# A two-block model on one core: first loads, mLSTM rows, modulation, norms, out-projections and the pooling row rearranged

## The chip, the cores and the metric

The kernel runs on one core of one Trainium2 chip. The metric is the device time of one execution in microseconds, the median of the runs. Three runs of the kernel before took 828.54, 823.75 and 828.04 us, so the median is 828.04. The trace that is read here is of another execution, which took 830.03 us; the span of its work is 828.2 us.

## The reference

The model takes `x` of 256 tokens by 1024 features through six layers, all in fp32, and ends with a norm. Every weight is read once.

```python
def first_block(x, ...):                      # two layers, plain residuals
    x = x + even_layer(rms_norm(x, norm_w[0]), ...)   # mLSTM (4 heads of 128) and sparse attention
    x = x + hgrn2_layer(rms_norm(x, norm_w[1]), ...)  # 8 gated recurrent heads of 128
def second_block(x, c, ...):                  # two layers, modulated by c
    c_act = jax.nn.silu(c)
    for i in range(2):
        mod = c_act @ ada_w[i] + ada_b[i]     # 1024 x 6144
        sh1, sc1, g1, sh2, sc2, g2 = jnp.split(mod, 6, axis=-1)
        h = modulate(rmsnorm(x, norm_mix_g[i]), sh1, sc1)
        x = x + g1 * (pool_mixer if i == 0 else sgu_mixer)(h, ...)
        h = modulate(rmsnorm(x, norm_mlp_g[i]), sh2, sc2)
        x = x + g2 * (jnp.square(jax.nn.relu(h @ w1)) @ w2)   # 1024 -> 4096 -> 1024
    return rmsnorm(x, final_g)
```

`even_layer` projects to some 4,400 columns and an out-projection of 1024 by 1024 ends it. The mLSTM works in chunks of 128 tokens; a product with exp(D - m) needs, for every head, the running maximum `m` and the summed gate `bcum`, one row of 256 numbers each, on all 128 partitions. The attention has 8 heads of 64 in two groups; its softmax rows are multiplied with the values of the selected blocks, of the window and of 15 compressed blocks. `pool_mixer` takes moving means over 2, 4, 8 and 16 tokens by four groups of 256 features and multiplies each group by a 256 by 256 matrix.

## The kernel before

**Tiles.** The residual stream `xT` lies with features on partitions: 8 tiles of 128 features by 256 tokens. A weight matrix is cut into pieces of 1024 by 128, laid out as 128x1024. SyncE's queue (SP) loads two of them at once (1 MB, `raw`, three buffers). Each fp32 piece is split (`split_w`, L155 to L163): ScalarE casts it to the matmul's rounded type (`whi`, L161), VectorE subtracts to get the low half (`wlo`, L162); four buffers each. Activations are split likewise into `ahi` and `alo` (or `num`, `nout`, `ghl`). A column tile is then 24 matmuls of 256 columns (`mm_T`, L221 to L223): hi by hi, hi by lo, lo by hi, for each of eight row tiles. Products that are not split run as plain fp32, two passes for each (x2 in the rows).

**Stages.** The even layer runs to about 208 us (35 column tiles in the order of the list `EV_TILES`, then an out-projection of 8 tiles), the recurrent layer to 343, pooling to 377, mlp0's two matrices to 465 and some 541, the sgu follows, then mlp1 from 637, then the last norm and four output transfers of 256 KB. In the even layer two generators, `mlstm` (one head a step) and `nsa` (the attention, in pieces), are called between column tiles with `run`, so that their work stands among the tiles' matmuls.

**Modulation.** `c_act @ ada_w` is done by VectorE: 96 loads of 512 KB (`araw`, two buffers, SP's queue), each reduced in one instruction against `row_c` (L351) into a column of `mod`, with a short read of the accumulator behind it. `ada` is a generator whose steps hold one or two of these; `step(upto)` issues the next one with a raised priority, `finish(upto)` all that are due. Calls of `step` stand in the stages by hand.

**Order.** A scheduler puts the instructions of each engine into a fixed order ahead of the run, by data dependencies, buffers and priorities; on the chip every engine works through its list and waits where an operand isn't there. PSUM has three banks for column tiles (`gbank`) and two for everything else (`mbank`).

**Places that the change touches.** The first loads stand at L106 to L109 and L175. A norm adds up seven squares on VectorE and sends two products of all ones through TensorE (L294). The mLSTM's selecting products read `mrow` and `bcum`, tensors of 4 partitions (L557, L559, L578); behind them come the mask products L558, L560 and the products by `ones` (L575, L588). The attention's products with the values are L776 (64 columns of weights for a group, so half of the array's columns) and L777 (compressed blocks): for one head in turn, all of group 0, then all of group 1. Pooling builds `prow`, a row of 1024 numbers on all partitions, with eight products over a broadcast of `mod` (L977) and four copies (L978); `pz` (L993) reads it, and the band product (L998) reads `pz`. In mlp1 the last column tile goes through the same code as the others: 512-column matmuls (hi and lo of the activation side by side, L1035), 256-column ones (L1036), and then two adds into `xT` (L330), the second of a copied half (L1041).

Of the kernel before, what the change touches and what calls it, by code (L numbers as in the profile page):

```python
# [8 lines left out]
F32 = mybir.dt.float32  # L9
# [9 lines left out]
T = 256  # L19
KT = 8  # L20
# [45 lines left out]
def tile_kernel(ctx: ExitStack, tc: tile.TileContext, io: dict, out: bass.AP):  # L66
# [37 lines left out]
    norm_w = mk(base, [128, 16], F32, "norm_w")  # L104
    xT = mk(base, [128, KT, T], F32, "xT")
    nc.scalar.dma_start(norm_w, io["norm_w"])  # L106

    def load_x(k):
        nc.sync.dma_start(xT[:, k : k + 2, :], io["xT"][k // 2].rearrange("p (k t) -> p k t", k=2))  # L109


# [53 lines left out]
    class Weights:  # L165
# [5 lines left out]
        def first(self, c0, c1, src):  # L171

            if not self.raw:
                self.raw[0] = mk(wpool, [128, 2048], F32, "raw", bufs=3)
            nc.scalar.dma_start(self.raw[0][:, c0:c1], src)  # L175

        def ahead(self, i, n):

            self.split = {i: self.piece(i, n, True)}
# [10 lines left out]
    def tile_T(ps, w, i, pair):  # L190

        wh, wl = w.piece(i, 128)
        mm_T(ps, lambda k: wh[:, k, :], lambda k: wl[:, k, :], pair.hi, pair.lo, range(KT))

# [60 lines left out]
    class Norm:  # L255
# [27 lines left out]
        def square(self, k, i=None):  # L283
# [3 lines left out]
            if i < KT - 1:  # L287
# [25 lines left out]
    def out_proj(src, pair, evict, side=0, every=1):  # L313
        w = Weights(lambda c: src[c])
        for n in range(8):
            if every and n % every == 0:
                step(side)
            ps = gbank()[:, :T]
            tile_T(ps, w, n, pair)
            evict(n, ps)  # L320
# [17 lines left out]
    def ada(crow):  # L338
# [19 lines left out]
    done = [0]  # L358
# [32 lines left out]
    def even_layer(norm, nxt, w):  # L391
        with ExitStack() as es:
# [65 lines left out]
            def columns(names):  # L458
                for name in names:
# [8 lines left out]
                    ps = gbank()[:, :T]  # L468
# [12 lines left out]
            columns(EV_TILES[:6])  # L481
# [14 lines left out]
            th = mk(wpool, [128, 1024], F32, "araw", bufs=2)  # L496
# [22 lines left out]
            out_proj(io["ev_w_out"], y, add_x(nxt), 5, 2)  # L519

    def mlstm(ev, et, qk, v, gsb, num, tanh):
# [10 lines left out]
        bc = mk(ev, [4, T], F32, "bcum")  # L532
# [3 lines left out]
        mr = mk(ev, [4, T], F32, "mrow")  # L536
# [12 lines left out]
        for h in range(H):  # L549
# [9 lines left out]
            PE.matmul(pb[:, 256:384], sel, mr[:, 128:256], start=True, stop=False)  # L559
# [18 lines left out]
            PE.matmul(pm[:, 0:T], sel, bc, start=True, stop=True)  # L578
# [18 lines left out]
    def nsa(ev, et, nqk, sv, gsb, cpair, nout):  # L597
# [111 lines left out]
        for qb in range(2):  # L709
# [33 lines left out]
            for j in range(4):  # L743
# [13 lines left out]
                for g in range(2):  # L757
                    for b in range(2):
# [3 lines left out]
                        else:  # L762
                            S.mul(x, x, r)
                    pt = mbank(0)
                    nb = qb + 1
# [6 lines left out]
                    dst = pov[64 * g : 64 * g + 64, j, :]  # L772
# [187 lines left out]
    def pool_layer(band, mod, norm, nxt):  # L960


        with ExitStack() as es:
# [7 lines left out]
            z = mk(pp, [128, 2, 1024], F32, "pz")  # L971
            for g in range(4):
                cs = slice(g * 256, g * 256 + 256)
                ps = mbank()[:, :256]
                for i in range(2):
                    k = 2 * g + i
                    PE.matmul(ps, mod[:, k : k + 1].to_broadcast([128, 128]), raw[:, k, :], start=i == 0, stop=i == 1)  # L977
                S.copy(row[:, cs], ps)  # L978
# [367 lines left out]
```

## Time and profile before

| | |
|---|---|
| median of three runs | 828.04 us |
| profiled execution | 830.03 us |
| its span | 828.2 us |
| TensorE busy | 807.2 us (97%), 6534 matmuls |
| weight loads | 740.2 us (89%) |
| VectorE | 672.1 us (81%) |
| ScalarE | 520.3 us (63%) |
| GpSimd | 4.9 us (1%) |
| DMA | 184.64 MB, mean 223 GB/s |

Matmuls are pipelined: a row's duration reaches into the next row's, so the price of one is the step from its start to the next start. "Idle before" is the time that an engine stood still ahead of a group, with what ended it. A chain of waits that goes back from the last instruction lies on TensorE for 66 per cent of the span, on DMA for 13 and on VectorE for 12.

### The profile page before, as it was taken

How to read it: one execution, taken by the hardware profiler on the slowest of the kernel's cores; microseconds unless marked ns; L12 is line 12 of the kernel's file. 1: busy time of each engine (PE TensorE's matmuls, PEld its weight loads, DVE VectorE, ACT ScalarE, POOL GpSimd, SP SyncE). 2: the span in 40 equal slices, each digit the busy share in tenths (PEclk: the TensorE clock that was granted, in tenths of full speed). 3: DMA queues.
4: the chain of work that ended last, by engine and by line, in shares of the span. 5: the costliest groups of instructions: out<-in, count | busy, mean ns of one | idle time of the engine just before them, and what ended most of it. 6: DMA issues, size and time to landing. Idle time of an engine off the chain costs nothing.

```text
span 828.2 us, 16357 instructions
## 1 busy us (share of the span) xinstructions
PE 807.2 (97%) x6534; PEld 740.2 (89%) x6534; DVE 672.1 (81%) x1257; ACT 520.3 (63%) x934; POOL 4.9 (1%) x19
## 2 busy tenths in 40 slices
PE   8999999989999999999999999999999999999995
PEld 8968977879999987999999888889999999988884
DVE  7689988899899989999999888876679777755552
ACT  7556765676876556658776734446657777754441
POOL 0000000001000000000000000000000000000000
PEclk9999999999999999999999999999999999999998
DMA  9644566657885777568878889874445454555521
GB/s 345 254 168 144 185 224 221 236 198 251 293 290 204 249 255 258 203 231 271 293 278 285 287 314 316 310 265 154 160 146 204 153 203 163 195 187 175 198 102 51
DMA packets 34635, 184.64 MB, mean 223 GB/s; under 512 B 3968, under 2 KB 4608, under 8 KB 19200
## 3 DMA queue, kind: packets, MB, share of 16 engines
q1 hardware_dynamic: 33696, 181.96, 62.8%
q10 hardware_dynamic: 864, 1.65, 0.6%
q8 instruction: 51, 0.84, 0.4%
q14 instruction: 24, 0.20, 0.1%
HBM read 182.55 MB, written 1.05 MB: 222 GB/s over the span
## 4 chain that ended last, share of the span: by engine, by line
PE 66%; DMA 13%; DVE 12%; ACT 5%; issue 4%; DVEq 0%; ACTq 0%; SPq 0%
PE g L221 12%; PE g L222 12%; DMA araw<-in_ada_w_dram 12%; PE g L223 12%; PE g L1035 9%; PE g L1036 5%; DVE wlo L162 4%; DVE araw L351 3%; ACT whi L161 2%; PE g L207 1%; PE g L208 1%; PE g L206 1%; PE m L858 1%; PE m L748 1%; PE long L776 1%
## 5 line engine op out<-in xcount | busy, mean ns | idle before, releaser
L221 PE MATMUL g<-ahi,whi 128*128 128x258 f32 (+1 forms) x1256 | 360.1, 289 | 4.0 <-ACT ahi L213 2.5
L222 PE MATMUL g<-alo,whi 128*128 128x258 f32 (+1 forms) x1256 | 357.6, 286 | 0.1
L223 PE MATMUL g<-ahi,wlo 128*128 128x258 f32 (+1 forms) x1256 | 356.6, 285 | 0.0
L162 DVE TENSOR_TENSOR wlo<-raw,whi 128x1024 fp32r<-128x1024 f32 (+1 forms) x238 | 288.6, 1216 | 73.5 <-ACT whi L161 72.9
L161 ACT CAST whi<-raw 128x1024 fp32r<-128x1024 f32 (+1 forms) x238 | 246.2, 1043 | 160.1 <-PE g L222 68.0
L221 PEld LDWEIGHTS g<-ahi,whi 128*128 128x128 f32 x1256 | 238.7, 191 | 8.7 <-ACT ahi L213 3.1
L222 PEld LDWEIGHTS g<-alo,whi 128*128 128x128 f32 x1256 | 240.2, 191 | 2.1 <-issue 0.8
L223 PEld LDWEIGHTS g<-ahi,wlo 128*128 128x128 f32 x1256 | 239.3, 191 | 1.7 <-issue 1.0
L1035 PE MATMUL g<-ghl,whi 128*128 128x512 f32 x512 | 179.9, 394 | 0.6 <-DVE nb L1020 0.6
L1036 PE MATMUL g<-ghl,wlo 128*128 128x256 f32 x512 | 143.5, 280 | 2.7 <-DVE wlo L162 2.4
L351 DVE CUSTOM_DVE_ANT_0 araw<-araw,row_c,prm 128x1024 f32<-128x1024 f32 x96 | 122.5, 1279 | 23.5 <-DMA araw<-in_ada_w_dram 23.3
L1035 PEld LDWEIGHTS g<-ghl,whi 128*128 128x128 f32 x512 | 96.0, 187 | 23.3 <-issue 0.7
L1036 PEld LDWEIGHTS g<-ghl,wlo 128*128 128x128 f32 x512 | 96.0, 187 | 4.0 <-DVE wlo L162 3.9
L310 DVE TENSOR_TENSOR nt<-g,nrstd 128x256 f32<-128x256 f32 x133 | 55.5, 419 | 17.3 <-PE g L223 16.9
L1021 ACT ACTIVATE nt<-nt,nb 128x256 f32<-128x256 f32 x64 | 32.4, 507 | 21.3 <-DVE nb L1020 21.3
L280 ACT ACTIVATE ahi<-xT,gains 128x256 fp32r<-128x256 f32 x32 | 16.2, 507 | 36.2 <-DVE xT L330 32.3
L214 DVE TENSOR_TENSOR ghl<-nt,ghl 128x256 fp32r<-128x256 f32 x64 | 27.0, 423 | 3.8 <-ACT ghl L213 1.4
L1022 ACT ACTIVATE nt<-nt 128x256 f32<-128x256 f32 x64 | 26.7, 418 | 1.9
L213 ACT CAST ghl<-nt 128x256 fp32r<-128x256 f32 x64 | 25.9, 406 | 1.9
L208 PE MATMUL g<-wlo,ahi 128*128 128x512 f32 (+1 forms) x64 | 24.3, 379 | 0.0
L206 PE MATMUL g<-whi,ahi 128*128 128x512 f32 (+1 forms) x64 | 24.2, 378 | 0.0
L286 ACT ACTIVATE sq<-xT 128x256 f32<-128x256 f32 x56 | 22.3, 405 | 3.0 <-DVE xT L330 3.0
(290 smaller groups left out, 758.7 us busy)
## 6 DMA issues: line engine op xcount, KB each, us to landing
raw<-in_mlp_w_dram SPq DMA_DIRECT2D x64, 1024.0 KB, 5.0
araw<-in_ada_w_dram SPq DMA_DIRECT2D x96, 512.0 KB, 5.1
raw<-in_ev_w_in_dram SPq DMA_DIRECT2D x17, 1024.0 KB, 6.1
raw<-in_od_w_in_dram SPq DMA_DIRECT2D x16, 1024.0 KB, 6.0
raw<-in_sgu_w_in_dram SPq DMA_DIRECT2D x8, 1024.0 KB, 4.7
raw<-in_ev_w_out_dram SPq DMA_DIRECT2D x4, 1024.0 KB, 4.9
raw<-in_od_w_out_dram SPq DMA_DIRECT2D x4, 1024.0 KB, 4.9
raw<-in_sgu_w_out_dram SPq DMA_DIRECT2D x4, 1024.0 KB, 4.7
```

The lines of the kernel that those rows point to most:

```text
L161: S.copy(hi[:, c], r[:, c])
L162: V.tensor_sub(lo[:, c], r[:, c], hi[:, c])
L206: PE.matmul(ps[tb], pair.hi(k)[:, ts_], wh[:, j, :], start=st, stop=False)
L208: PE.matmul(ps[tb], pair.hi(k)[:, ts_], wl[:, j, :], start=False, stop=sp)
L221: PE.matmul(ps, wh(k), ah(k), start=st, stop=False)
L222: PE.matmul(ps, wh(k), al(k), start=False, stop=False)
L223: PE.matmul(ps, wl(k), ah(k), start=False, stop=sp)
L310: V.tensor_tensor(t, ps[:, :T], self.r, op=ALU.mult)
L351: V.tensor_tensor_reduce(raw, raw, crow, 1.0, P("ada_b", layer * 48 + c), ALU.mult, ALU.add, mod[:, c : c + 1])
L1021: S.activation(r, r, AF.Relu, bias=b)
L1035: PE.matmul(ps, wh[:, k, :], a.rearrange("p s t -> p (s t)"), start=st, stop=sp, skip_group_check=True)
L1036: PE.matmul(ps[:, :T], wl[:, k, :], a[:, 0, :], start=False, stop=sp, skip_group_check=True)
```

## The change

It has ten parts. (1) First loads: the weight halves of tiles 0 and 1 go by SP's queue, `x` with `norm_w` in front of it (one tensor `xn`) mostly by ScalarE's; tiles 1 and 2 are split ahead, and tiles 3 to 5 take `mbank`s. (2) `mrow` and `bcum` become 128 partitions high, zeros below the fourth, and the selecting products read all of them. (3) The attention's value products alternate between the two groups, the compressed blocks first. (4) Norms with a pair of operands add all eight squares on VectorE and send one product; the last norm keeps two. (5) An out-projection's first three tiles are done by row halves, in three banks, and no modulation step stands in it. (6) Modulation steps are called by a table of positions, `PACE`, in the mlps and the sgu, with three `araw` buffers. (7) An attention step moves ahead of four of the even layer's column tiles. (8) The pooling row is made by column-tiled products (32 columns of weights each, four side by side), copied once and spread over the partitions by four transfers on ScalarE's queue; the first band product takes 144 columns for 256. (9) mlp1's last tile is done by `mm_T`, without the copied half and the second add. (10) The output transfers alternate between SP's and ScalarE's queues.

```diff
+    def load_x(queue, k):
+        a = 0 if k == 0 else 16 + k * T
+        queue.dma_start(xn[:, a : 16 + (k + 2) * T], io["xn"] if k == 0 else io["xT"][k // 2 - 1])
+    def tiles_T3(ps, w, i, pair):
+        ws = [w.piece(i + j, 128) for j in range(3)]
+        for ks in (range(4), range(4, 8)):
+            for j in range(3):
+                wh, wl = ws[j]
+                mm_T(ps[j], ..., pair.hi, pair.lo, ks, ks[0] == 0, ks[0] == 4)
-                if i < KT - 2:
+                if i < KT - 1 - two:
-            PE.matmul(self.ps, ones, sq, start=i == KT - 2, stop=i == KT - 1)
+            PE.matmul(self.ps, ones, sq, start=i == KT - 2 or not two, stop=i == KT - 1)
-                        raw = mk(wpool, [128, 1024], F32, "araw", bufs=2)
+                        raw = mk(wpool, [128, 1024], F32, "araw", bufs=3)
+    PACE = ((0, 30), (256, 36), (512, 60), (640, 66), (704, 66), (960, 72))
+    def pace(tiles):
+        u = done[1]
+        done[1] += tiles
+        for (u0, s0), (u1, s1) in zip(PACE, PACE[1:]):
+            if u0 <= u < u1:
+                while done[0] * (u1 - u0) < s0 * (u1 - u0) + (s1 - s0) * (u - u0):
+                    step(12)
-            columns(EV_TILES[25:31])
+            columns(EV_TILES[25:27])
+            run(ns)
+            columns(EV_TILES[27:31])
...
-            run(ns)
-            out_proj(io["ev_w_out"], y, add_x(nxt), 5, 2)
+            out_proj(io["ev_w_out"], y, add_x(nxt))
+        bc128, mr128 = [mk(ev, [128, T], F32, t) for t in ("bcum", "mrow")]
+        G.memset(bc128, 0.0)
+        G.memset(mr128, 0.0)
-            sel = ident[0:4, h : h + 1].to_broadcast([4, 128])
+            sel = ident[:, h : h + 1].to_broadcast([128, 128])
-            PE.matmul(pb[:, 0:T], sel, mr, start=True, stop=False)
+            PE.matmul(pb[:, 0:T], sel, mr128, start=True, stop=False)
-                    for b in range(2):
-                        for i in range(nb):
-                            PE.matmul(dst, vv, pT[:, b, i, :], start=b == 0 and i == 0, stop=False, skip_group_check=True)
-                    PE.matmul(dst, vcp[:, g, j, :], ptc[:, g, :], start=False, stop=True, skip_group_check=True)
+                for g in range(2):
+                    PE.matmul(pov[64 * g : 64 * g + 64, j, :], vcp[:, g, j, :], ptc[:, g, :], start=True, stop=False, skip_group_check=True)
+                for b in range(2):
+                    for i in range(nb):
+                        for g in range(2):
+                            PE.matmul(pov[64 * g : 64 * g + 64, j, :], vv, pTs[g][:, b, i, :], start=False, stop=b == 1 and i == nb - 1, skip_group_check=True)
-                    PE.matmul(ps, mod[:, k : k + 1].to_broadcast([128, 128]), raw[:, k, :], start=i == 0, stop=i == 1)
-                S.copy(row[:, cs], ps)
+                    PE.matmul(ps[32 * g : 32 * g + 32], mod[:, k : k + 1].to_broadcast([128, 32]), raw[:, k, :], start=i == 0, stop=i == 1, tile_position=(0, 32 * g))
+            S.copy(row4, ps)
+                nc.scalar.dma_start(row[:, g * 256 : g * 256 + 256], row4[32 * g : 32 * g + 1, None, :].to_broadcast([1, 128, 256]))
-                PE.matmul(ps, z[:, 0, n * 128 : n * 128 + 128], m[:, 0:256], start=True, stop=False)
+                PE.matmul(ps[:, 0:144], z[:, 0, n * 128 : n * 128 + 128], m[:, 0:144], start=True, stop=False, skip_group_check=True)
-                if layer == 0 and n % 2 == 0:
-                    step(11)
-                if layer and n % 4 == 3:
-                    step(12)
+                pace(8)
+                    if layer and n == 7:
+                        mm_T(ps[:, :T], ..., range(8), first=c == 0, last=c == 3)
+                        continue
+    w.first(nc.sync, 0, 512, io["ev_w_0"][0])
+    load_x(nc.scalar, 0)
+    w.first(nc.sync, 512, 1024, io["ev_w_0"][1])
+    load_x(nc.scalar, 2)
+    load_x(nc.sync, 6)
+    load_x(nc.scalar, 4)
+    w.first(nc.sync, 1024, 2048, io["ev_w_1"])
-        nc.sync.dma_start(out[:, k : k + 2, :], x)
+        (nc.scalar if k % 4 else nc.sync).dma_start(out[:, k : k + 2, :], x)
```

What the scheduler makes of it is seen in the engines' lists. The first place is VectorE in the even layer, ahead of the low half `wlo_1715`, the 27th piece's (`araw` rows are modulation's reductions, `nmx` and `nsm` the attention's softmax, `w`, `qk` and `cpt` the mLSTM's). Before:

```order
L351 ISA araw_1333,mod_10_89<-araw_1333,row_c_396,prm_71 128x1024
L351 ISA mod_10_89 128x1
L162 TENSOR_TENSOR wlo_1715<-raw_1263,whi_1714 128x1024
L310 TENSOR_TENSOR nt_1293<-g_1262,nrstd_164 128x256
L569 SCALAR_TENSOR_TENSOR mE_1308<-m_231_1311,mE_1308 128x384
```

In the change:

```order
L787 RECIPROCAL nsm_892<-nsm_892 128x4
L615 TENSOR_TENSOR w_263_1447<-w_262_1445,w_263_1447 128x256
L788 TENSOR_TENSOR nsm_892<-nsm_892,gtok_703 128x4
L367 ISA araw_1620,mod_9_87<-araw_1620,row_c_394,prm_71 128x1024
L367 ISA mod_9_87 128x1
L793 TENSOR_SCALAR A_1376<-A_1376,nsm_892 128x128 x2
L621 SCALAR_TENSOR_TENSOR cpt_225_1296<-w_263_1447,m_265_1453 128x256
L586 SCALAR_TENSOR_TENSOR qk_181<-w_285_1533,qk_181 128x256
L586 SCALAR_TENSOR_TENSOR qk_181<-w_286_1536,qk_181 128x256
L757 TENSOR_REDUCE nmxc_1462<-m_272_1464 128x8
L163 TENSOR_TENSOR wlo_1715<-raw_1263,whi_1714 128x1024
```

`wlo_1715` was VectorE's instruction 169 and is now its 212th; between it and the piece before (`wlo_1266`) stand 11 reductions, where 3 stood.

The second place is TensorE at the attention's products with the values (`nPT` are the transposed softmax weights of one group, `sv` the values, `vcp` the compressed values; `m` and `kblk` belong to the scores of the next head). Before:

```order
L222 MATMUL g_1745<-alo_114,whi_1748 128x256
L776 MATMUL long_915<-nPT_1358,sv_175 64x128 x2
L777 MATMUL long_915<-nPtc_913,vcp_696 64x128
L776 MATMUL long_915<-nPT_1368,sv_175 64x128 x2
L777 MATMUL long_915<-nPtc_913,vcp_696 64x128
```

In the change:

```order
L814 MATMUL long_915<-nPT_1360,sv_183 64x128
L780 MATMUL m_247_1377<-kblk_663,nqk_185 128x256
L814 MATMUL long_915<-nPT_1365,sv_183 64x128
L814 MATMUL long_915<-nPT_1360,sv_183 64x128
L814 MATMUL long_915<-nPT_1365,sv_183 64x128
L781 LDWEIGHTS identbf_80
L781 MATMUL m_247_1377<-nnegbf_558,identbf_80 128x256
L780 MATMUL m_248_1384<-kblk_663,nqk_185 128x256
L781 LDWEIGHTS identbf_80
L781 MATMUL m_248_1384<-nnegbf_558,identbf_80 128x256
L809 MATMUL long_915<-nPtc_913,vcp_694 64x128 x2
```

The two groups' products now stand by turns, here with one of the next head's scores between the first two; the two compressed products in the last row open the next head.

The third place is VectorE in pooling, from the last residual add of the recurrent layer's out-projection (`xT`, now `xn`) to the first `pz`. Before:

```order
L324 TENSOR_TENSOR xT_73<-xT_73,g_4443 128x256
L277 TENSOR_TENSOR alo_4625<-mod_10_89,ahi_4624 128x4x2
L162 TENSOR_TENSOR wlo_4727<-raw_4687,whi_4726 128x1024
L281 SCALAR_TENSOR_TENSOR alo_4363<-xT_73,gains_11_90,ahi_4362 128x256
L351 ISA araw_5416,mod_12_91<-araw_5416,row_c_396,prm_71 128x1024
L351 ISA mod_12_91 128x1
L351 ISA araw_5495,mod_12_91<-araw_5495,row_c_396,prm_71 128x1024
L351 ISA mod_12_91 128x1
L305 COPY rcol_4519<-m_713_4516 128x2
L993 SCALAR_TENSOR_TENSOR pz_4499<-g_4521,rcol_4519,prow_4498 128x256 x2
```

In the change:

```order
L163 TENSOR_TENSOR wlo_4726<-raw_4680,whi_4725 128x1024
L290 SCALAR_TENSOR_TENSOR alo_4363<-xn_72,gains_10_88,ahi_4362 128x256
L299 TENSOR_TENSOR sq_4473<-sq_4473,sq_4438 128x256
L367 ISA araw_6160,mod_11_89<-araw_6160,row_c_394,prm_71 128x1024
L367 ISA mod_11_89 128x1
L367 ISA araw_6183,mod_11_89<-araw_6183,row_c_394,prm_71 128x1024
L367 ISA mod_11_89 128x1
L163 TENSOR_TENSOR wlo_4765<-raw_4762,whi_4764 128x1024
L316 COPY rcol_4518<-m_710_4515 128x2
L367 ISA araw_6208,mod_11_89<-araw_6208,row_c_394,prm_71 128x1024
L367 ISA mod_11_89 128x1
L1033 SCALAR_TENSOR_TENSOR pz_4499<-g_4520,rcol_4518,prow_4498 128x256 x2
```

The add itself (of `xn`) and one more `alo` stand just ahead of these rows. One sum of squares, one low half and one reduction have come in between.

## Rows read from the trace of the kernel before

**Rows 1.** Busy time by stage, with the granted clock as a share of full speed.
```profile
core 0: us, PE busy (x) PEld busy (x) DVE busy (x) ACT busy (x) POOL busy (x), PEclk, DMA share, GB/s
92.00:208.00 116.00, 113.51 (x816) 97.89 (x814) 104.55 (x239) 77.98 (x193) 2.92 (x4) 0.99 0.64 219
208.00:343.00 135.00, 133.30 (x1719) 122.32 (x1720) 127.88 (x223) 89.53 (x147) 0.00 (x0) 1.00 0.73 250
343.00:377.00 34.00, 33.80 (x250) 31.84 (x249) 32.72 (x67) 20.78 (x45) 0.00 (x0) 1.00 0.70 240
377.00:465.00 88.00, 87.41 (x711) 85.86 (x710) 80.78 (x166) 65.38 (x120) 0.00 (x0) 1.00 0.81 286
465.00:541.00 76.00, 73.34 (x414) 62.93 (x413) 63.69 (x94) 35.10 (x50) 0.00 (x0) 1.00 0.88 309
```

**Rows 2.** TensorE's waits: what for, us in total, times, longest.
```profile
PE g L221 <- ACT ahi L213: 2.5, 3, 1.7
...
PE g L1036 <- DVE wlo L162: 2.4, 2, 1.4
```

**Rows 3.** Timeline of the start: start, duration, instruction, idle time before.
```profile
7.30 0.62 ACT L161 CAST whi<-raw 128x512 fp32r<-128x512 f32 x1 [1.45 <-DMA raw<-in_ev_w_dram]
```

**Rows 4.** Timeline of TensorE around one mLSTM head.
```profile
108.11 0.60 PE L574 MATMUL m<-mE,ones 128*128 128x256 f32 x2
108.55 0.39 PE L575 MATMUL m<-mE,ones 128*128 128x128 f32 x2
108.86 0.69 PE L578 MATMUL m<-bcum,cst 4*128 4x256 f32 x2
109.49 0.39 PE L221 MATMUL g<-ahi,whi 128*128 128x256 f32 x1
...
110.90 0.66 PE L588 MATMUL m<-w,ones 128*128 128x256 f32 x2
111.49 0.69 PE L557 MATMUL m<-mrow,cst 4*128 4x256 f32 x2
112.11 0.23 PE L558 MATMUL m<-mnegbf,identbf 128*128 128x128 bf16 x1
112.27 0.48 PE L559 MATMUL m<-mrow,cst 4*128 4x128 f32 x2
112.69 0.23 PE L560 MATMUL m<-mnegbf,identbf 128*128 128x128 bf16 x1
```

**Rows 5.** Timeline of TensorE at the attention's products with the values.
```profile
144.14 1.09 PE L776 MATMUL long<-nPT,sv 128*64 128x128 f32 x8
...
146.05 0.38 PE L777 MATMUL long<-nPtc,vcp 128*64 128x128 f32 x2
```

**Rows 6.** TensorE's groups, 92 to 190 us: busy us, mean ns, idle before.
```profile
L776 PE MATMUL long<-nPT,sv 128*64 128x128 f32 x88 | 10.6, 281 | 0.0
...
L777 PE MATMUL long<-nPtc,vcp 128*64 128x128 f32 x28 | 5.1, 273 | 0.0
```

**Rows 7.** Timeline of TensorE at products of 32 columns of weights.
```profile
48.35 1.08 PE L643 MATMUL m<-raw,cX 128*32 128x128 f32 x32 [1.18 <-issue]
```

**Rows 8.** VectorE's groups, 92 to 190 us: modulation's reductions.
```profile
L351 DVE CUSTOM_DVE_ANT_0 araw<-araw,row_c,prm 128x1024 f32<-128x1024 f32 x23 | 29.4, 1278 | 2.0 <-DMA araw<-in_ada_w_dram 2.0
```

**Rows 9.** Modulation's tile `araw`, 92 to 190 us: the issues on SP, the landing.
```profile
L350 SPq DMA_DIRECT2D araw<-in_ada_w_dram x22: 327/328/328, 96.3 to 188.5; - x22
...
DMA to landing us min/median/max: 3.2/4.5/7.5
```

**Rows 10.** Timeline at pooling.
```profile
352.97 1.89 PE L977 MATMUL m<-raw,mod 128*128 128x256 f32 x8
...
353.51 0.41 DVE L324 TENSOR_TENSOR xT<-xT,g 128x256 f32<-128x256 f32 x1
...
358.63 0.48 DVE L993 SCALAR_TENSOR_TENSOR pz<-g,rcol,prow 128x256 f32<-128x256 f32 x1 [0.62 <-PE g L991]
```

**Rows 11.** Timeline of VectorE at the end.
```profile
819.29 0.48 DVE L330 SCALAR_TENSOR_TENSOR xT<-g,mod,xT 128x256 f32<-128x256 f32 x1 [8.20 <-ACT nt L1041]
819.81 0.48 DVE L330 SCALAR_TENSOR_TENSOR xT<-nt,mod,xT 128x256 f32<-128x256 f32 x1
```

More of the change, by code (lines that the diff above doesn't have):

```diff
@@ L169, in __init__, with first, ahead @@
             self.src, self.raw, self.split = src, {}, {}
-        def first(self, c0, c1, src):
+        def first(self, queue, c0, c1, src):
             if not self.raw:
                 self.raw[0] = mk(wpool, [128, 2048], F32, "raw", bufs=3)
-            nc.scalar.dma_start(self.raw[0][:, c0:c1], src)
-        def ahead(self, i, n):
-            self.split = {i: self.piece(i, n, True)}
+            queue.dma_start(self.raw[0][:, c0:c1], src)
+        def ahead(self, i, n, halves=False):
+            self.split[i] = self.piece(i, n, halves)
         def piece(self, i, n, halves=False):
@@ L286, in square @@
             S.activation(sq, xT[:, k, :], AF.Square)
-            if i < KT - 1:
+            two = self.pair is None
+            if i < KT - 1 or not two:
                 if self.acc is not None:
@@ L311, in scaled, with out_proj @@
             return t
-    def out_proj(src, pair, evict, side=0, every=1):
+    def out_proj(src, pair, evict, side=0, every=0):
         w = Weights(lambda c: src[c])
+        three = [gbank()[:, :T] for _ in range(3)]
+        tiles_T3(three, w, 0, pair)
         for n in range(8):
@@ L317, in out_proj @@
                 step(side)
+            if n < 3:
+                evict(n, three[n])
+                continue
             ps = gbank()[:, :T]
@@ L480, in even_layer @@
             early = []
-            columns(EV_TILES[:6])
+            columns(EV_TILES[:3])
+            columns(EV_TILES[3:6], mbank)
             after(V.tensor_tensor(gbias, P("ev_b", b0), P("f_bias"), op=ALU.add), [norm.last])
@@ L577, in mlstm @@
             pm = mbank(1)
-            PE.matmul(pm[:, 0:T], sel, bc, start=True, stop=True)
+            PE.matmul(pm[:, 0:T], sel, bc128, start=True, stop=True)
             e2 = mk(et, [128, T], F32, "w1", bufs=4)
@@ L1028, in mlp @@
                 for c in range(4):
-                    if layer == 0 and c % 2 == 0:
-                        step(11)
+                    pace(8)
                     wh, wl = w2.piece(4 * n + c, 128)
+                    if layer and n == 7:
+                        mm_T(ps[:, :T], lambda k: wh[:, k, :], lambda k: wl[:, k, :], lambda k: g[:, 8 * c + k, 0, :],
+                             lambda k: g[:, 8 * c + k, 1, :], range(8), first=c == 0, last=c == 3)
+                        continue
                     for k in range(KT):
@@ L1039, in mlp @@
                 add = scaled_add(mod[:, 40:48])
-                lo = mk(tmp, [128, T], F32, "nt", bufs=3)
-                S.copy(lo, ps[:, T:])
                 add(n, ps[:, :T])
-                add(n, lo)
+                if n < 7 or not layer:
+                    lo = mk(tmp, [128, T], F32, "nt", bufs=3)
+                    S.copy(lo, ps[:, T:])
+                    add(n, lo)
                 if layer == 0 and n == 5:
@@ L1078, in gelu_tile @@
             def gelu_tile(dst, n):
-                step(11)
+                pace(8)
                 ps = gbank()[:, : norm.pair.w]
@@ L1125, in sgu_layer @@
             out_proj(io["sgu_w_out"], y, scaled_add(mod[:, 16:24], nxt))
+            pace(64)
     w = Weights(lambda c: io["ev_w_in"][c - 1])
     warm(9)
-    for i in range(4):
-        load_x(2 * i)
-        if i < 2:
-            w.first(512 * i, 512 * i + 512, io["ev_w_0"][i])
-    w.first(1024, 2048, io["ev_w_1"])
+    w.first(nc.sync, 0, 512, io["ev_w_0"][0])
[5 more added lines that the diff above has]
+    w.first(nc.sync, 1024, 2048, io["ev_w_1"])
     nc.sync.dma_start(prm, io["prm"])
@@ L1139, in tile_kernel @@
         if k == 1:
-            w.ahead(0, 128)
+            w.ahead(0, 128, True)
+    w.ahead(1, 128)
     for k in range(KT):
         n0.square(k)
+        if k == 3:
+            w.ahead(2, 128)
     n1 = Norm(norm_w[:, 8:16])
```

44 lines of the change are left out of this document (23 added, 21 removed).

## The prediction

> **What bounds the kernel now.** I read the busy time of the engines by stage first [rows 1]. In every stage from 92 to 541 us TensorE is covered for 96 to 99 per cent of the time, at full granted clock, so time that leaves its stream can come off the end. The same rows say what stands behind it: VectorE covers 104.55 of 116 us in the even layer's second half (90 per cent), 127.88 of 135 in the recurrent layer (95) and 32.72 of 34 around pooling (96). A TensorE that becomes faster there meets VectorE after 11.4, 7.1 and 1.3 us. The list of TensorE's waits comes next [rows 2]: two kinds are touched by the change, the wait for the first activation half-split of an out-projection (2.5 us in three places) and for a low half of weights in the second matrix of mlp0 (2.4 us in two). Then come the timelines at the places that are edited, since a group's mean duration of a pipelined matmul says nothing of its price; the step from one start to the next does.
>
> **The change, part by part.** The sum is made against the profiled execution of 830.0 us, which stands 2.0 above the median of the runs.
>
> *Start.* The second half of tile 0's weights is waited for: ScalarE sat 1.45 us until it landed and cast it at 7.30 [rows 3]. With the weight halves on one queue and x on the other, I take 1.4 off. The bounds are 0 (the same bytes have to come first) and -3.0 (the wait shortened twice over, since tiles 1 and 2 are split ahead as well). The Trainium skill, "DMA: Bandwidth & Descriptors", section "Issuing engines are not separate DMA queues", speaks against it: transfers issued by different engines run on the same 16 engines and interleave, so only issue time is saved. By that rule the start and the split output transfers give nothing, and the sum would be 1.4 higher; no row of before shows two queues in a race for one tile, so I keep the bound.
>
> *mLSTM rows.* The selecting products read 4 partitions. From one start to the next the 256-column one of L578 takes 0.63 us (108.86 to 109.49), where the 256-column product over 128 partitions of L574 takes 0.44 (108.11 to 108.55) [rows 4]. There L557 takes 0.62 and the 128-column L559 0.42, against 0.44 and half of it. The product beside such a one pays too: L588 0.59 for 0.44, L575 0.31 for 0.22, L558 0.16 for the 0.06 that its size suggests. Over 128 partitions a head saves 0.19 + 0.18 + 0.20 + 0.15 + 0.09 + 0.10 = 0.9. Four heads give 3.6, of which 0.5 lies before 92 us. The two memsets that fill the padding run on GpSimd, busy 2.92 us of 116 [rows 1], and cost nothing.
>
> *Attention products.* The 64-column products stand in runs of one half: 18 passes between 144.14 and 146.05, 0.106 us each [rows 5]. There are 88 + 28 = 116 of them [rows 6], 12.3 us. The order now alternates the halves. That column tiles can run side by side shows in the 32-column products: 32 passes of 128 columns in 1.08 us, 0.034 each [rows 7]. So a pair costs one, and 6.2 us go; the bounds are 0 and 6.2.
>
> *Out-projections.* Three tiles by row halves let TensorE start on the first four operands. The even layer's wait is the longest of the three, 1.7; the other two share 0.8, of which I take 0.6 at the sgu [rows 2].
>
> *Norms.* Six norms lose one product of 256 columns, 0.44 (L574 in [rows 4]), and gain an add of 0.41 on VectorE (like L324 in [rows 10]): -0.4 each, two of them behind 541 us.
>
> *Modulation.* The 96 reductions are not spread evenly by the new table: in the changed order 25 lie in the even layer's tiles (20 before), 1 in its out-projection (4), 30 in the recurrent layer (28), 25 in mlp0's first matrix (23), 14 in the second (20). What matters is the burst on VectorE between the low halves wlo_1266 and wlo_1715, where 11 stand for 3. At 1.28 us each [rows 8] they are 14.1 us; the other work there adds 14.4, by the durations of the same instructions before (all of them among the 239 of [rows 1]). TensorE's work between its uses of the two pieces comes to 17.9, so VectorE's lead shrinks by 10.6, where it shrank by 3.7 (12.4 against 8.7). Adding up both engines from the start, VectorE comes to that stretch some 4.7 us ahead of its closest point. That leaves 6 us in which TensorE waits for wlo_1715, since hardly a tile's matmul is left to fill it. Queued behind the burst on SP is the weight load raw_1936, which waits for its buffer anyway. The attention step that moved ahead of four column tiles, and the other banks of tiles 3 to 5, are in these sums of the order.
>
> So **92 to 208 us**: TensorE loses 3.1 + 6.2 + 1.7 + 0.4 = 11.4, and 6.0 comes back: **-5.4**. The bounds are -8.4 (VectorE's 104.55, two more reductions and an add leave 8.4 of the 116 us [rows 1]) and 0.
>
> **Recurrent layer**: a norm product less, two more reductions of 1.28 on an engine with 7.1 us to spare. +0.6, bounds -0.4 and +2.6. **Pooling**: 16 passes of 0.22 us for the row (eight in 1.89 with the last one's tail, [rows 10]) become 16 that overlap by fours, -2.6; the narrower band products save 112 of 256 columns eight times, 1.5; one norm product 0.4. But `pz` is behind more on VectorE: between the last residual add (353.51) and `pz` (358.63) lay 5.1 us [rows 10], and the new order puts one more reduction, one more low half, which takes about as long, and an add there, some 3 us. I take 0, bounds -4.5 and +3. The row's four transfers have those 8 us; the modulation loads landed in 4.5 at the median, 7.5 at most [rows 9]. **mlp0's first matrix**: two reductions more, +0.5 (0 to +2.6). **Its second matrix**: six fewer, 7.7 us of VectorE, on which the 2.4 us of waits [rows 2] rest: -2.2 (0 to -2.7, the uncovered time there [rows 1]).
>
> **The end.** Without the low half of the last tile its copy and the second add go, at 819.29 one add and one of the same size behind it [rows 11]: -0.9 with the copy. The output's four transfers now go by two queues; at 0.33 us an issue [rows 9] that is between 0 and -0.7, and I take 0, because each waits for its own scaled piece. The last tile's 96 narrow products in place of 64 mixed ones, +0.2. With two norms (-0.9) and the sgu's start (-0.6): -2.2.
>
> Sum: -1.4 - 0.4 (first norm) - 0.5 (first head) - 5.4 + 0.6 + 0 + 0.5 - 2.2 - 2.2 = **-11.0**, 819.0 in a profiled execution and **817** at the median.
>
> **The rivals.**
>
> *All of it comes off.* If the scheduler's burst is absorbed and VectorE follows, TensorE's whole removal counts: start -3.0, first norm and head -0.9, even layer -11.4, recurrent layer -0.4, pooling -4.5, mlp0 -2.7, the end -2.2, together -25.1: 803. For it speaks the coverage of 96 to 99 per cent; against it the 8.4 us that VectorE leaves in the even layer, and the burst. Chance 0.17.
>
> *VectorE is the bound already.* A matmul's record overlaps the next, so 113.51 of 116 may overstate TensorE; by weight loads it is at 97.89 (84 per cent), below VectorE's 90 [rows 1]. Then what leaves TensorE between 92 and 541 us returns nothing, four norm adds cost 1.7 there, and only the start, the first norm and the end count: -1.4 - 0.4 - 2.2 + 1.7 = -2.3, so 826 at the median. Against it: the lists show TensorE's starts packed at a matmul's own step [rows 4], which a starved engine would not have. The Trainium skill, "Perfetto Trace Analysis", section "Identifying the Most-Contended Engine", says just this: matmul busy time is no measure of the bound, weight-load time is, and VectorE is judged by its occupancy. By that page this rival would be the forecast. Chance 0.22.
>
> *The burst starves on its transfers: slower.* Eleven reductions run through three buffers, so eight loads wait for a reduction before. A buffer's turn is its landing time, 1.28 for the reduction and 0.33 for the issue [rows 9]; 8/3 turns fill the 28.5 us of VectorE work at a landing of 9.1 us. Beyond that each further us costs 2.7, and TensorE, with no tile at hand, waits along. At 15 us it is +16: 833, and up to 850. Loads landed in 7.5 at most [rows 9], so 0.06.
>
> *It doesn't do what it says.* The halves of the attention products may not run side by side, since an instruction of another kind stands between some pairs: 6.2 comes back, 823. The 32-column products speak against it. Chance 0.07.
>
> *The forecast* keeps 0.48, with a range of its own of 811 to 823.
>
> **The numbers.** Two in ten are left out by 803 to 828: half of the first rival, the upper third of the second, most of the third. One per cent of 828 is 8.3 us, about what this kernel's runs can tell from nothing. Faster than 819.8: some 0.36 of the forecast's 0.48, all of the first rival, a little of the rest, 0.55. Slower than 836: the upper half of the burst rival, 0.04. Within: 0.41.
>
> **What would show it.** Right: between 92 and 208 us TensorE's stream is about 11 us shorter, with one gap of some 6 us ahead of the matmuls on wlo_1715 and VectorE at reductions in it; L578's successor steps by 0.44; 116 passes take about 6 us; no wait for a low half in mlp0's second matrix. Wrong: no such gap (first rival), many small gaps for VectorE in the even layer (second), reductions that wait for their loads (third), passes still 0.106 apart (fourth). Were pooling's row to wait for its transfers, `pz` would be released by a DMA.

## The result, and the profile after

The changed kernel takes 835.55 us (median of six runs, 835.06 to 838.06) against 828.77 for the kernel before (six runs): a ratio of 1.0096, with a 95% interval of 1.0068 to 1.0123. It is slower by 6.8 us where I had forecast 11 us less. The page of its profiled execution:

```profile
span 833.9 us, 16394 instructions
...
PE 797.4 (96%) x6554; PEld 731.2 (88%) x6554; DVE 672.8 (81%) x1262; ACT 520.7 (62%) x930; POOL 5.4 (1%) x21
...
PE   8998989999999999949999999999999999999995
```

TensorE works 9.8 us less than before (797.4 against 807.2), and the span is 5.6 us longer: 15 us of new idle time. The strip of 40 slices says where most of it is, the 4 in the 19th slice. The stages, to be set against [rows 1] (busy time, granted clock, DMA share):

```profile
92.00:208.00 116.00, 110.90 (x812) 93.02 (x811) 108.14 (x246) 78.92 (x194) 2.92 (x4) 1.00 0.68 237
208.00:343.00 135.00, 134.47 (x1737) 123.59 (x1736) 131.80 (x231) 91.01 (x149) 0.00 (x0) 1.00 0.75 266
343.00:382.00 39.00, 26.62 (x198) 25.05 (x197) 26.93 (x59) 14.79 (x35) 0.00 (x0) 0.87 0.59 150
382.00:465.00 83.00, 81.41 (x666) 80.21 (x665) 81.45 (x166) 64.68 (x114) 0.00 (x0) 1.00 0.86 308
465.00:545.00 80.00, 80.00 (x483) 70.95 (x482) 64.98 (x97) 41.61 (x61) 0.00 (x0) 1.00 0.77 281
```

Around pooling TensorE is covered for 26.62 of 39 us, where it was 33.80 of 34, and the granted clock is 0.87. TensorE's longest waits, to be set against [rows 2]:

```profile
PE m L314 <- ACT nrstd L407: 5.8, 1, 5.8
PE m L1039 <- DVE xn L346: 4.7, 1, 4.7
PE m L769 <- DVE nEc L766: 2.6, 1, 2.6
PE g L232 <- DVE wlo L163: 2.4, 3, 1.4
PE m L620 <- ACT w L618: 2.1, 1, 2.1
PE m L1039 <- DVE pz L1033: 1.9, 1, 1.9
```

The first two and the last are in pooling, 12.4 us together. The waits for `nEc` (a product of the attention, `cst` by `nEc`) and for `w` (the mLSTM's) are in the even layer. The timeline of ScalarE there (queue rows are `ACTq`):

```profile
351.54 0.37 ACT L1016 COPY prow<-m 128x256 f32<-128x256 f32 x1
...
351.95 0.55 ACTq L1018 DMA_DIRECT2D prow<-prow  x1
...
352.54 7.81 ACTq L1018 DMA_DIRECT2D prow<-prow  x3
360.39 0.47 ACT L407 ACTIVATE nrstd<-m,eps 128x256 f32<-128x256 f32 x1 [7.77 <-issue]
```

Three issues of the row's transfers hold ScalarE for 7.81 us, and the norm's square root behind them starts 7.77 us late: that is the first wait. The other two in pooling are seen on VectorE, which needs the row itself:

```profile
364.25 1.65 DVE L1033 SCALAR_TENSOR_TENSOR pz<-g,rcol,prow 128x256 f32<-128x256 f32 x4
368.52 0.88 DVE L1033 SCALAR_TENSOR_TENSOR pz<-g,rcol,prow 128x256 f32<-128x256 f32 x2 [2.62 <-DMA prow<-prow]
373.02 0.88 DVE L1033 SCALAR_TENSOR_TENSOR pz<-g,rcol,prow 128x256 f32<-128x256 f32 x2 [3.63 <-DMA prow<-prow]
```

The wait that is put down to `xn` is in truth one for the last transfer: VectorE did `pz` at 373.02 and `xn` right behind it. Lined up by the same matmul of TensorE in both, in the first tiles of each stage, the two traces stand like this (us; what a row gains is counted from the row above):

| stage begins | before | after | difference | gained since the row above, forecast | measured |
|---|---|---|---|---|---|
| recurrent layer | 213.4 | 212.1 | -1.2 | -7.7 | -1.2 |
| its out-projection | 330.3 | 329.0 | -1.3 | +0.6 | -0.1 |
| mlp0, first matrix | 377.6 | 388.7 | +11.1 | 0 | +12.4 |
| mlp0, second | 472.5 | 482.4 | +10.0 | +0.5 | -1.1 |
| sgu | 568.2 | 574.1 | +5.8 | -2.2 | -4.2 |
| end of the span | 828.2 | 833.9 | +5.6 | -2.2 | -0.2 |

### The profile page after: what moved, and what is told of

It is laid out like the page before. It is cut to its first block, busy times and chain, and to the rows that moved or that the text cites. A ratio compares the mean times of both kernels' runs of the same rounds, so it can differ in the third digit from the quotient of the medians.

```text
span 833.9 us, 16394 instructions
## 1 busy us (share of the span) xinstructions
PE 797.4 (96%) x6554; PEld 731.2 (88%) x6554; DVE 672.8 (81%) x1262; ACT 520.7 (62%) x930; POOL 5.4 (1%) x21
## 4 chain that ended last, share of the span: by engine, by line
PE 81%; DVE 9%; ACT 4%; DMA 4%; issue 2%; ACTq 0%; DVEq 0%
PE g L230 16%; PE g L232 16%; PE g L231 16%; PE g L1077 13%; PE g L1078 7%; DMA prow<-prow 2%; DVE wlo L163 2%; DVE araw L367 1%; PE m L780 1%; ACT whi L162 1%; PE long L814 1%; PE g L215 1%; PE g L216 1%; PE g L217 1%; DVE hk L944 1%
## 5 line engine op out<-in xcount | busy, mean ns | idle before, releaser
L230 PE MATMUL g<-ahi,whi 128*128 128x258 f32 (+1 forms) x1232 | 350.9, 287 | 4.6 <-ACT whi L162 1.9
L232 PE MATMUL g<-ahi,wlo 128*128 128x258 f32 (+1 forms) x1232 | 348.0, 284 | 2.5 <-DVE wlo L163 2.4
L231 PE MATMUL g<-alo,whi 128*128 128x258 f32 (+1 forms) x1232 | 348.9, 284 | 0.3
L231 PEld LDWEIGHTS g<-alo,whi 128*128 128x128 f32 x1232 | 233.2, 189 | 2.9 <-issue 1.6
L232 PEld LDWEIGHTS g<-ahi,wlo 128*128 128x128 f32 x1232 | 232.3, 189 | 4.0 <-DVE wlo L163 3.3
L1077 PE MATMUL g<-ghl,whi 128*128 128x512 f32 x480 | 168.1, 393 | 0.0
L1078 PE MATMUL g<-ghl,wlo 128*128 128x256 f32 x480 | 133.9, 279 | 0.0
L295 ACT ACTIVATE sq<-xn 128x256 f32<-128x256 f32 x56 | 22.5, 406 | 19.5 <-DVE xn L346 19.1
L289 ACT ACTIVATE ahi<-xn,gains 128x256 fp32r<-128x256 f32 x32 | 16.2, 506 | 17.9 <-DVE xn L346 17.7
L346 DVE SCALAR_TENSOR_TENSOR xn<-g,mod,xn 128x256 f32<-128x256 f32 x24 | 11.6, 482 | 16.2 <-PE g L232 9.5
```

The source lines that it names most:

```text
L230: PE.matmul(ps, wh(k), ah(k), start=st, stop=False)
L231: PE.matmul(ps, wh(k), al(k), start=False, stop=False)
L232: PE.matmul(ps, wl(k), ah(k), start=False, stop=sp)
L1077: PE.matmul(ps, wh[:, k, :], a.rearrange("p s t -> p (s t)"), start=st, stop=sp, skip_group_check=True)
L1078: PE.matmul(ps[:, :T], wl[:, k, :], a[:, 0, :], start=False, stop=sp, skip_group_check=True)
```

## The experiments

Each ratio is against the kernel before, run on the same chip in between. "Changed" is the changed kernel.

**1. The old pooling row in the changed kernel.**

```diff
-  PE.matmul(ps[32 * g : 32 * g + 32], ..., tile_position=(0, 32 * g))   # and one copy, four transfers
+  PE.matmul(ps, mod[:, k : k + 1].to_broadcast([128, 128]), raw[:, k, :], ...)   # and four copies
```

> The changed kernel with the pooling row made as before (eight products over 128 columns, four copies, no transfers); everything else stays. Theory 1, the row's four transfers are what makes the change slower: between the pooling products and mlp0 the changed kernel loses 16.2 us against the kernel before, so this run comes out at 835.5 - 16 = 819 us, and TensorE's waits of 5.8 us for the norm and of 4.7 and 1.9 us for the band products are gone. Rival, the loss there comes from VectorE's longer list ahead of pz (3 us by my estimate) and the rest from elsewhere: about 832.

828.65 us, ratio 0.9997 (0.997 to 1.0024). The three waits are gone and the stage is back to its old length (-0.4 us from the out-projection to mlp0, +12.4 in changed). But 7 us came back, not 16. Part of the rest went at another place: in this profiled execution the stretch from 120 to 145 us ran at a lower clock than in changed (first this run, then changed):

```profile
120.00:145.00 25.00, 22.71 (x117) 18.16 (x116) 18.25 (x43) 12.11 (x40) 0.00 (x0) 0.80 0.56 190
```

```profile
120.00:145.00 25.00, 22.43 (x147) 17.52 (x147) 22.25 (x49) 14.77 (x45) 0.00 (x0) 1.00 0.67 230
```

The mean of 0.80 lies between TensorE's levels of 2.4 and 1.2 GHz, so for part of this stretch it ran at the lower one; ahead of it stands the idle time of the burst of reductions (9.18 us covered of 110 to 120). In changed the same 9.18 stand there and the clock stayed at 1.00, so that this idle time alone makes the clock fall is not shown. TensorE is 1.1 us behind changed at 99 us and 5.2 at 142. Over this kernel's ten runs the time follows the clock: 823.44 to 825.59 us where the mean granted clock is 0.993 or more, 827.83 to 832.03 where it is 0.984 to 0.988.

**2. The row's transfers issued by SyncE.**

```diff
-                nc.scalar.dma_start(row[:, g * 256 : ...
+                nc.sync.dma_start(row[:, g * 256 : ...
```

> The changed kernel with the row's four transfers issued by SyncE instead of ScalarE. Theory 1a, ScalarE is held by its own issues (7.8 us for three of them) and everything that it does next is late: the norm's square root comes some 8 us sooner, its wait of 5.8 us on TensorE is gone, and 6 to 8 us of the 16 come back: 828. Theory 1b, the landing of the transfers (7.0 to 17.4 us) bounds the stage whoever issues them: the norm comes sooner too, but the last pz still waits until some 17 us after the copy, and the time stays at 833 to 836.

836.25 us, 1.0092 (1.0062 to 1.0121): nothing comes back (1b). ScalarE is free and its wait is gone, yet `pz` waits 10.5 us in four places for the row, and the issues hold SyncE for up to 4.80 us as they held ScalarE for up to 4.78. What bounds the stage is when the row lands:

```profile
DMA to landing us min/median/max: 7.1/12.9/16.0
```

In changed that row reads

```profile
DMA to landing us min/median/max: 7.0/13.4/17.4
```

**3. The new row alone in the kernel before** (the same diff as 1, the other way).

> The kernel before with the new pooling row alone (column-tiled products, one copy, four transfers by ScalarE's queue). Theory 1: the loss belongs to this one edit and shows alone, 14 to 18 us slower than before, 843 to 847. Rival, it takes the other edits with it (two more modulation loads in flight with three buffers, ScalarE's other work): 829 to 836.

842.41 us, 1.0166 (1.0131 to 1.02): this one edit costs 14.7 us by itself. Here ScalarE is not held: the four issues take 0.48 to 0.61 us each. Yet the transfers land no sooner, and `pz` waits 13.7 us for them:

```profile
DMA to landing us min/median/max: 8.7/13.5/17.8
```

**4. Two buffers for modulation's loads, with the old row.**

```diff
-                        raw = mk(wpool, [128, 1024], F32, "araw", bufs=3)
+                        raw = mk(wpool, [128, 1024], F32, "araw", bufs=2)
```

> The changed kernel with the old pooling row, and two buffers for the modulation's loads instead of three. The list of VectorE then has 4 reductions ahead of wlo_1715 where the changed kernel has 11. Theory 2, the burst of reductions costs the even layer what I forecast (6 us of idle TensorE; the traces show its idle time in this layer 5.3 us longer than before): 5 us below the kernel with the old row and three buffers, about 814. Rival, the idle time only moves (the reductions have to be done somewhere on an engine that is 90 per cent busy there): within 1 us of it.

824.93 us, 0.9958 (0.9932 to 0.9984), 3.7 below run 1, where 5 were expected. The products on `wlo_1715` itself start at 110.1 us, as before the change (109.8), where they start at 127.5 in changed, most of that behind other work that TensorE does first. The idle time between 92 and 150 us is gone (0.07 us here, 3.17 in run 1), but between 150 and 208 it is 3.78 for 1.70: two thirds of it only moved, as the rival has it. The other difference that the two traces show is the granted clock between 92 and 150, 1.00 here and 0.91 in run 1. The two intervals overlap, so the size is rough; the direction is as forecast.

**5. The row from 32 partitions.** All 32 partitions of a column group hold the same numbers, so 32 rows can be read from 32 places.

```diff
-  nc.scalar.dma_start(row[:, cols], row4[32 * g : 32 * g + 1, None, :].to_broadcast([1, 128, 256]))
+  for r in range(4):
+      (nc.sync if r % 2 else nc.scalar).dma_start(row[32 * r : 32 * r + 32, cols], row4[32 * g : 32 * g + 32, :])
```

> The changed kernel, but the pooling row is spread by 16 transfers of 32 rows, each row from a partition of its own (all 32 partitions of a column group hold the same numbers), half of them issued by SyncE and half by ScalarE. Still 512 rows of 1 KB. In the changed kernel the row's queue took 39.9 per cent of 16 engines over 23 us for 576 packets, 0.25 us each, and the whole moved 27 to 36 GB/s for 6 us. Theory 1c, rows that all come from one partition are what is slow: the last pz comes some 8 us sooner, 824 to 829. Rival 1d, 512 small packets are slow wherever they come from, or wait behind the weights' and modulation's loads of these microseconds: the last transfer lands 13 us or more after the copy and the time stays at 833 to 838.

829.16 us, 1.0013 (0.9988 to 1.0037), as with the old row. The last `pz` starts at 366.3 us, 7.1 sooner than in changed. The landing:

```profile
DMA to landing us min/median/max: 1.7/2.4/6.4
```

**6. The same 16 transfers, each from one partition.**

```diff
-  ..., row4[32 * g : 32 * g + 32, :])
+  ..., row4[32 * g : 32 * g + 1, None, :].to_broadcast([1, 32, 256]))
```

> As the run with 16 transfers of 32 rows from 32 partitions, with the one difference that all 32 rows of a transfer are read from one partition, as in the changed kernel; sizes, number of transfers and queues stay. There the transfers landed in 1.7 to 6.4 us (7.0 to 17.4 in the changed kernel) and the time was 829.2. Theory 1c, reading one partition again and again is slow: transfers land in 8 us or more and the time is back at 833 to 838. Rival 1e, what helped was the cut into 16 transfers on two queues: 827 to 831 again.

835.65 us, 1.0089 (1.0059 to 1.0119). Between this run and the one before only the place that is read differs, and the whole loss is back. The landing is 4.4/6.5/7.7 us, a little under my 8. The DMA view of 23 us around pooling shows the price; q10 is ScalarE's queue (packets, MB, share of 16 engines). With 32 partitions, then with one:

```profile
q10 hardware_dynamic: 384, 0.26, 4.0%
```

```profile
q10 hardware_dynamic: 384, 0.26, 20.0%
```

Of the 384 packets 256 are the rows of 1 KB (eight transfers of 32); the others have 4 bytes each. A row took 0.040 x 16 x 23 / 256 = 0.06 us of one engine, and now 0.29. In changed it is 512 rows and 39.9 per cent, again 0.29 us each.

**7. The attention's products in one run a head, in the kernel before.**

```diff
+  # after both groups' transposes
+  for b in range(2):
+      for i in range(nb):
+          for g in (1, 0):     # the group that is ready last goes first
+              PE.matmul(pov[64 * g : 64 * g + 64, j, :], vv, pTs[g][:, b, i, :], start=b == 0 and i == 0, ...)
+  for g in range(2):
+      PE.matmul(pov[64 * g : 64 * g + 64, j, :], vcp[:, g, j, :], ptc[:, g, :], start=False, stop=True, ...)
```

> The kernel before with this one edit, the attention's products by turns and in one run a head. If the halves run side by side whenever they stand together: 12.89 us become 9.0, 3 to 4 us faster than before, 824. Rival, the second group's transposes are now waited for by the first group's products too: within 1 us of before.

824.61 us, 0.9964 (0.9943 to 0.9986). Summing the steps from the first product of a run to the matmul behind it, all 128 passes take 12.9 us before (9 runs), 12.5 in changed (24 runs) and 8.2 here (8 runs). TensorE in changed, at one of its short runs:

```profile
104.71 0.43 PE L814 MATMUL long<-nPT,sv 128*64 128x128 f32 x2
105.07 0.39 PE L231 MATMUL g<-alo,whi 128*128 128x256 f32 x1
```

and here:

```profile
142.08 1.09 PE L780 MATMUL long<-nPT,sv 128*64 128x128 f32 x16
143.00 0.39 PE L782 MATMUL long<-nPtc,vcp 128*64 128x128 f32 x4
143.32 0.28 PE L749 MATMUL m<-nnegbf,identbf 128*128 128x256 bf16 x1
```

Two passes that stand alone cost 0.36 us (104.71 to 105.07), twenty together 1.24 (142.08 to 143.32). Before the change, group by group, twenty took 1.95 to 2.23.

**8. The same order of products with the old row and two buffers, in changed.**

```diff
-                for g in range(2):
-                    PE.matmul(pov[64 * g : 64 * g + 64, j, :], vcp[:, g, j, :], ptc[:, g, :], start=True, ...)
-                        for g in range(2):
+                        for g in (1, 0):
...
+                for g in range(2):
+                    PE.matmul(pov[64 * g : 64 * g + 64, j, :], vcp[:, g, j, :], ptc[:, g, :], start=False, stop=True, ...)
```

> The kernel with the old pooling row and two buffers for modulation, and the attention's products with the values in one run a head: the group whose transposed weights come last goes first, the compressed blocks last, so that nothing stands between. In the changed kernel's trace 128 passes in 24 runs take 12.45 us where 9 runs took 12.89 before: a run of 2 passes takes 0.36, one of 14 takes 1.02. By these a run of 12 takes 0.91 and one of 20 takes 1.35, 9.0 in all: 3.4 us less, 821.5 against 824.9 without it. Rival, the longer wait for both groups' transposes opens a gap ahead of each run and nothing is won: 824 to 826.

822.38 us, 0.9936 (0.9907 to 0.9964), 2.5 below run 4, where 3.4 were expected; the intervals overlap.

**9. mLSTM's rows on 128 partitions alone, in the kernel before.**

```diff
+        bc128, mr128 = [mk(ev, [128, T], F32, t) for t in ("bcum", "mrow")]    # zeros below row 3
-            sel = ident[0:4, h : h + 1].to_broadcast([4, 128])
+            sel = ident[:, h : h + 1].to_broadcast([128, 128])
-            PE.matmul(pm[:, 0:T], sel, bc, start=True, stop=True)
+            PE.matmul(pm[:, 0:T], sel, bc128, start=True, stop=True)
```

> The kernel before with the mLSTM's rows on 128 partitions alone. I priced it at 3.6 us on TensorE. If this stands on TensorE's path: 3 to 4 us faster than before, 824. Rival, VectorE paces the even layer where these products stand and only part of it comes: 0 to 2 us faster.

825.56 us, 0.9972 (0.9954 to 0.9991). The row that answers to L578 in [rows 4], and the next:

```profile
107.97 0.60 PE L580 MATMUL m<-bcum,cst 128*128 128x256 f32 x2
108.22 0.47 PE L221 MATMUL g<-ahi,whi 128*128 128x256 f32 x1
108.52 0.28 PE L222 MATMUL g<-alo,whi 128*128 128x256 f32 x1
```

The pair with L221 takes 0.55 us, where it took 0.85 (108.86 to 109.71 in that trace). Over a head it is 0.9 less, as priced. The time fell by 2.4 us, between the 3 to 4 of the forecast and the 0 to 2 of the rival.

**10 to 12. Towards a faster version:** 7 and 9 together; with the first loads and the last tile of the change; with one product a norm and the narrower band product as well. The lines of the last two beside those of 7 and 9:

```diff
+    w.first(nc.sync, 0, 512, io["ev_w_0"][0])      # and the other first loads as in the change
+                    if layer and n == 7:
+                        mm_T(ps[:, :T], ...)           # 11 and 12: the last tile
-            PE.matmul(self.ps, ones, sq, start=i == KT - 2, stop=i == KT - 1)
+            PE.matmul(self.ps, ones, sq, start=i == KT - 2 or not two, stop=i == KT - 1)   # 12 only
-                PE.matmul(ps, z[:, 0, n * 128 : n * 128 + 128], m[:, 0:256], start=True, stop=False)
+                PE.matmul(ps[:, 0:144], z[:, 0, n * 128 : n * 128 + 128], m[:, 0:144], ...)    # 12 only
```

> The kernel before with two edits, mLSTM's rows on 128 partitions and the attention's products by turns in one run a head. Alone they gave 2.4 and 3.3 us. If both stand on TensorE's path they add up: 5 to 6 us faster than before, 822. Rival, VectorE, 90 per cent busy there, takes part of the second back: 2 to 4 us.

> The kernel before with four edits: those two, the ordered first loads and the last tile without its low half (outputs by one queue, as before). In the changed kernel's trace the sixth tile came 2.0 us sooner but the twelfth only 0.6, and from the last matmul to the last add it took 0.92 us less. So 1 to 2 us on top of the two edits: 820 to 821. Rival, the start's gain is lost again at the twelfth tile and nothing is added: 822.

> As the one with four edits, and two more: one product of ones a norm with one more add, and the narrower first band product. By TensorE's steps these take 5 x 0.4 and 1.5 us more off: 817 if they stand on its path. Rival, at the norms TensorE waits for the last square and its chain, so that the product saved is replaced by an add of the same length, and pooling is paced by VectorE: no change, 820 to 821.

820.11 us (0.9912, 0.9881 to 0.9942), 819.37 (0.9906, 0.9879 to 0.9932) and 819.73 (0.9907, 0.9884 to 0.993). The first two edits give 7.9 us (the interval runs from 4.8 to 9.9; 5 to 6 were expected), near the 4.7 and 3.6 that they take from TensorE's steps; nothing that can be measured comes from the other four. Run 11 doesn't show what the start alone is worth: without the change's banks for tiles 3 to 5 TensorE waits 1.11 and 1.07 us for the first norm at 18 to 21 us, and the sixth tile's low half comes at 27.1, later than before (26.0; 24.0 in changed). All three runs beat both kernels, by 0.9 per cent of the kernel before.

## Why the prediction was wrong

**The step that failed is pooling**, where I wrote "The row's four transfers have those 8 us; the modulation loads landed in 4.5 at the median, 7.5 at most" and took 0 with a bound of +3. The transfers landed in 7.0 to 17.4 us and the stretch up to mlp0 grew by 12.4, of the 16.6 us between the forecast and the profiled execution. I priced a transfer by another of larger size and left out what differs: 128 rows all read from one partition. Runs 5 and 6 show that this is the cause. The 4.5 was also taken from another stage: around pooling (351 to 374 us) modulation's loads landed in 8.0 at the median before the change. Runs 2 and 3 show that ScalarE's 7.8 us under its own issues, which I hadn't counted either, did not matter beside it. The prediction did name the sign, `pz` released by a DMA, but gave it no rival and no chance.

**The attention's products were mis-sized**: 6.2 us forecast, 0.4 measured. Halves side by side is right (8.2 in run 7), but I had the order in front of me, with scores between the pairs, and priced it as if each pair stood in a long run. It was listed as a rival with 0.07; it had to be the forecast, since a short run's fixed cost eats the gain.

**The burst** came, but not as forecast: 6.0 us in one gap ahead of the products on `wlo_1715`. In changed TensorE is idle for 3.4 us between 92 and 150 us (none before), and it waits at the mLSTM's products, 0.77 us for `qk` at 113.97 and 2.09 for `w` at 122.20, which VectorE reaches late between the reductions; at `wlo_1715` it doesn't wait. Over the even layer its idle time grew from 7.4 to 12.7 us, 5.3 more, which looks like the 6.0 by luck: 2.2 of it is the wait for `nEc`, 2.59 us at 82.57 where it was 0.43, ahead of the burst and the same with two buffers. A lower clock behind the burst, as in run 1's trace, was not in the sum. The loads did not starve: between 92 and 208 us they landed in 3.1, 4.2 and 6.5 us (least, median, most) and no reduction waited. The slower rival (833 up to 850) holds the measured 835.55, but not by its mechanism.

**mLSTM's rows** were right in size (0.9 a head). **VectorE is the bound already** is excluded for the even layer as a whole: runs 7, 9 and 10 take work from TensorE alone there and are faster by 3.3, 2.4 and 7.9 us. In single places it holds (`nEc`, below), and the other stages were not tested. On this the Trainium skill's page "Perfetto Trace Analysis" (section "Identifying the Most-Contended Engine") pointed the other way here: VectorE had the higher occupancy (90 per cent between 92 and 208 us, weight loads 84), yet the time went with TensorE's steps.

**The start** gave 2.0 us at the sixth tile and 0.6 at the twelfth, for 1.4 forecast. Of the 2.3 us that the sum takes off ahead of 92 us nothing is left at the product with `nEc`: it starts at 82.57, before at 82.40, after the same work but for one norm product, because TensorE waits 2.59 us there for VectorE's chain. So it didn't come off the end, and the even layer's gains were small: 1.2 us in all up to the recurrent layer, for 7.7 forecast. **The out-projection's** wait of 1.7 us for its operands is gone, but one of 1.42 for a low half stands there instead (188.63 us). **mlp0** gave more than forecast, 1.1 and 4.2 us. With the old row the second matrix gives back as much (-4.2 in run 1's trace), so it isn't the pooling delay coming back; that the six fewer reductions do it all was not tried apart. **The end** gave 0.2 for 2.2. In the changed kernel's tail

```profile
824.69 0.48 DVE L346 SCALAR_TENSOR_TENSOR xn<-g,mod,xn 128x256 f32<-128x256 f32 x1 [8.70 <-PE g L232]
...
828.09 1.59 SPq L1215 DMA_DIRECT2D out_dram<-xn  x2
828.69 1.55 ACTq L1215 DMA_DIRECT2D out_dram<-xn  x2
```

the last matmul starts at 824.37 and the final square at 825.21, 0.84 later (1.76 before: 818.57 and 820.33), so the second add's 0.9 came. But from the first output transfer to the end it is 5.79 us (828.09 to 833.88), before the change 5.03 (823.21 to 828.24). The second queue is not the cause: run 11 sends all four transfers by one queue, also out of `xn`, and takes 5.55. Its output transfers and those of the kernel before (by one queue, out of `xT`) land like this:

```profile
DMA to landing us min/median/max: 2.4/2.7/2.8
```

```profile
DMA to landing us min/median/max: 2.1/2.3/2.4
```

In changed it is 2.4/2.7/2.9. Why transfers out of `xn` land later is not shown. The Trainium skill, "DMA: Bandwidth & Descriptors" (section "Issuing engines are not separate DMA queues"), says that a second issuing engine saves only the time of the issue; the end agrees, with 2.7 us to landing at the median by two queues and by one, and the start can't tell, since tiles 1 and 2 were split ahead there as well. The norms' products saved gave nothing (run 12).

What stays open: how far the clock, and not the burst's idle time, sets the difference between runs 1 and 4, since it varies from execution to execution, and what makes it fall in one and not in another.

## What to carry to other kernels

Price a transfer by what it reads and how, not by its size: a row spread over 128 partitions from one partition took three times as long to land (13.4 us at the median) as a load of four times its bytes (4.5 [rows 9]). Read the order between two instructions that are to overlap before booking the gain, and book a short run at its own price (0.36 us for two passes). Time saved on TensorE can be lost again at the next product that waits for another engine (here 2.59 us at `nEc`). A local stall can have a second price where TensorE's clock falls after it, as in run 1's trace.

## What was not expected of the hardware

- Rows of 1 KB read from one partition took 0.29 us of a DMA engine each (changed and run 6), from 32 partitions 0.06 (run 5).
- While such transfers were under way the issuing engine was held for up to 4.8 us an issue, on ScalarE (changed) and on SyncE (run 2) alike, against 0.33 for modulation's loads [rows 9]. In run 3 the same issues took 0.61 at most; what decides it is not shown.
- A run of 64-column products costs 0.36 us for 2 passes and, with the halves by turns, 1.24 for 20.
